# A Mamba skip weight loaded as a row, and dense feed-forward products of 512 columns with one loaded weight part

## The chip, the cores and the metric

The kernel runs on one core of one Trainium2 chip. The metric is device time in microseconds (us), the median of several runs. A core has five engines with an instruction queue each: TensorE (PE; its weight loads are shown apart as PEld), VectorE (DVE), ScalarE (ACT), GpSimd (POOL) and SyncE (SP, which here only issues transfers). Each queue is worked off in order; semaphores order the engines among each other. Sixteen DMA engines carry the transfers of all queues.

## The reference, cut to what matters

The program is two stacked blocks of two layers each on 256 tokens of width 1024. The change touches the three dense feed-forward layers (two in the first block, one in the second, all with a hidden width of 2816) and one vector of the Mamba layer.

```python
def swiglu_ffn(h, norm, w13, w2):                 # first block, both layers
    u = rms_norm(h, norm) @ w13
    return (silu(u[..., :2816]) * u[..., 2816:]) @ w2

def swiglu(h, w_gate, w_up, w_down):              # second block, first layer
    return (silu(h @ w_gate) * (h @ w_up)) @ w_down

# inside mamba2_mixer: ssm_d has 32 values, one for each head of 64 channels
    y = y + xf * d_skip[:, None]
```

All operands are 32-bit floats.

## The kernel before

**Split products.** TensorE works here in a rounded 32-bit format (fp32r), so each operand is split in a high part (rounded) and a low part (what the rounding left). `weights` (line 213) loads up to 128x2048 weights in one transfer of 1 MB from SP's queue into a buffer `raw`, then makes `wh` with four casts of 512 columns on ACT (line 227) and `wl` with four subtractions on DVE (line 228). `mm3` (lines 239 to 244) makes one product of the split operands as three: high weights by high operand (L242), high weights by low operand (L243), low weights by high operand (L244). Each of the three loads its 128x128 weights anew and passes 256 columns (the tokens) through them. I call the three a triple.

**A dense layer** (`ffn`, line 449). For each of 11 values of j, 256 hidden channels are made: `proj_fm` through `proj_steps` (line 249) for the gate weights, then for the up weights. Each such group is one `weights` call and 2 x 8 triples (two halves m of 128 channels, eight blocks k of the width) into one PSUM bank (`pa`, four banks of 512 columns; a group fills one). Then DVE multiplies gate and up by the row norm (`fg` L463, `fu` L465, both read PSUM), ACT makes the silu (L464), DVE the product (L466), and `split` makes `hidH` (ACT, L301) and `hidL` (DVE, L304). `out_proj` (line 379) then goes over four pairs of output blocks: 2 x 22 triples into one bank, one DVE addition of 512 columns to the residual `hT` (L395), and `norm_block` for the next layer. So a dense layer has 11 x 2 x 2 x 8 = 352 triples in gate and up and 4 x 2 x 22 = 176 in the output product: 528 in all, 1584 in the three layers.

**The normed operand.** `norm_block` (line 317) keeps the normed operand as tiles `xH` and `xL` of two blocks each; ACT writes `xH` (L326), DVE writes `xL` (L327).

**Buffers.** `wh` and `wl` have three buffers each in the dense layers and `raw` four (the `wider` context in `run`), so the parts of a third group can be made once the first group's triples have ended.

**The start.** `transpose_in` loads x, then SP issues the first weights of the even layer (`in_ev_w_in`). On POOL's queue `mamba_load` (line 646) loads three vectors of 32 values: two as rows broadcast to 128 partitions (L653) and the skip weight `ssm_d` as columns: `dcol` holds for 16 pairs of heads one head's value in the partitions 0 to 63 and the other's in 64 to 127, by two transfers (L657) that read 16 values at a stride of two for each of 64 partitions. `dcol` is first used in the Mamba layer (L777).

The order of the instructions on each engine is set by the framework's scheduler from priorities, when the program is built; it is not written out by hand.

Of the kernel before, what the change touches and what calls it, by code (L numbers as in the profile page):

```python
# [21 lines left out]
T = 256  # L22
# [28 lines left out]
def wait(tasks):  # L51
    while not all(t.done for t in tasks):
        yield


class Core:
# [192 lines left out]
    def proj_steps(s, src, c0, cn, X, evac, nk=8, tasks=None):  # L249
# [3 lines left out]
        while cn > 0:  # L253
            n = min(cn, 256)
            w = s.weights(src, 0, nk, c0, n)
            p = s.psum("a")
            nm = (n + 127) // 128
            for m in range(nm):
                mc = min(128, n - m * 128)
                for k in range(nk):  # L260
# [46 lines left out]
    def norm_open(s, gain, k0=0):  # L307
# [3 lines left out]
        N.H, N.L = [], []  # L311
        N.X = s.of_pairs(N.H, N.L)
# [4 lines left out]
    def norm_block(s, N, d0, src=None):  # L317
# [3 lines left out]
        N.H.append(s.t2([128, 2, T], "xH", F32R))  # L321
        N.L.append(s.t2([128, 2, T], "xL", F32R))
        for m in range(2):
            g = s.col(N.gain, N.k0 + d0 + m)
# [54 lines left out]
    def out_proj(s, src, Y, nk, nxt):  # L379

        moe = nxt == "moe"
        N = s.moe_open() if moe else s.norm_open(*nxt) if nxt else None
        block = s.moe_block if moe else s.norm_block
        for dp in range(4):
            p = s.psum("a")
            for k0 in range(0, nk, 8):
                n = min(8, nk - k0)
                w = s.weights(src, 128 * k0, n, dp * 256, 256)
                for m in range(2):
                    for k in range(n):  # L390
                        kk = k0 + k
                        s.mm3(p[:, m * 256:m * 256 + 256], [t[:, k, m * 128:m * 128 + 128] for t in w], Y(kk),
                              start=(kk == 0 and m == 0), stop=(kk == nk - 1))
            h = s.hT[:, 2 * dp:2 * dp + 2, :]
            s.nc.vector.tensor_add(h, h, p.rearrange("p (m t) -> p m t", m=2))  # L395
# [53 lines left out]
    def ffn(s, N, gate, up, gc, uc, w2, nxt):  # L449
# [4 lines left out]
        hH, hL = [], []  # L454
# [3 lines left out]
        for j in range(0, nf, 2):  # L458
            res = {}
            s.proj_fm(gate, gc + j * 128, 256, X, lambda _, p, n: res.__setitem__("g", p))  # L460
            s.proj_fm(up, uc + j * 128, 256, X, lambda _, p, n: res.__setitem__("u", p))
# [5 lines left out]
            hH.append(s.t2([128, 2, T], "hidH", F32R))  # L467
            hL.append(s.t2([128, 2, T], "hidL", F32R))
            s.split(u, hH[-1], hL[-1])
        return s.out_proj(w2, s.of_pairs(hH, hL), nf, nxt)  # L470
# [136 lines left out]
class Mamba:  # L607
# [38 lines left out]
    def mamba_load(s):  # L646
# [3 lines left out]
        vb = s.cp.tile([128, 2, 32], F32, name="ssmvb")  # L650
        for m, nm in enumerate(("ssm_dt_bias", "ssm_a_log")):
# [3 lines left out]
        sd = I["ssm_d"]  # L655
        for m in range(2):
            nc.gpsimd.dma_start(dcol[m * 64:m * 64 + 64],  # L657
# [1819 lines left out]
```

## Time and profile before

| | |
|---|---|
| median of 3 runs | 2528.38 us (2525.06 to 2529.42) |
| the profiled execution, its own time | 2530.27 us |
| span of its instructions | 2528.2 us |
| PE busy | 2329.6 us (92%) |
| the three dense layers, PE's stretch | about 382 to 574, 840 to 1030 and 1140 to 1328 us |
| PE's first product of weights | at 35.61 us |

The profile is of one execution. Its page gives busy time by engine, the span in 40 slices and the chain of work that ended last. The trace behind it is asked in views: instructions by line, a stretch in order of time, busy time by stretch, the transfers, and all instructions that touch one tile. A row with brackets says how long its engine sat idle ahead of it and what ended that. The time of a matmul includes its way through the array, so two neighbours overlap: the distance between two starts is what one costs in a full queue.

### The profile page before, as it was taken

To read this page: it belongs to the slowest core of one execution; us is meant where nothing else is said; L and a number is where in the kernel's file an instruction comes from. 1 tells how busy PE (TensorE), PEld (TensorE's weight loads), DVE (VectorE), ACT (ScalarE), POOL (GpSimd) and SP (SyncE) were. 2 spreads that over 40 slices of the span, in tenths; PEclk is the share of its full clock that TensorE was granted. 3 is DMA by queue.
4 is the path that set the end of the run, shared out by engine and by line. 5 is a ranking of instruction groups with operands and counts; after the bars stand their busy time and mean duration, and the time that the engine had idled before them with its cause. 6 is when DMAs were issued, how large, how long until landed. Compare 5 with 4: busy or idle time off the path is not lost.

```text
span 2528.2 us, 38949 instructions
## 1 busy us (share of the span) xinstructions
PE 2329.6 (92%) x15366; PEld 1917.4 (76%) x15366; DVE 1575.5 (62%) x2924; ACT 1201.5 (48%) x2075; POOL 88.3 (3%) x179
## 2 busy tenths in 40 slices
PE   4988999999998999989999998999999998788786
PEld 4877889999888999879999898787878883222222
DVE  4786677658986765766658885888888871000000
ACT  3554465445654544664446552777777661000000
POOL 3010110000001000000000000000000000000000
PEclk9998999999999999989999998999999999999999
DMA  6322245555434555515554300999999989999998
GB/s 116 118 77 68 74 161 174 175 183 156 134 117 151 152 177 178 177 58 184 182 169 151 101 18 31 376 343 355 359 357 343 345 308 412 410 411 410 411 412 319
DMA packets 266190, 559.55 MB, mean 221 GB/s; under 512 B 12751, under 2 KB 172510, under 8 KB 251662
## 3 DMA queue, kind: packets, MB, share of 16 engines
q1 hardware_dynamic: 264544, 555.71, 61.4%
q0 software_dynamic: 1328, 1.22, 1.0%
q8 instruction: 123, 2.02, 0.3%
q14 instruction: 69, 0.57, 0.1%
q10 hardware_dynamic: 126, 0.03, 0.0%
HBM read 555.88 MB, written 1.05 MB: 220 GB/s over the span
## 4 chain that ended last, share of the span: by engine, by line
PE 67%; DMA 14%; DVE 6%; ACT 3%; issue 2%; POOL 1%; SPq 0%; POOLq 0%; ACTq 0%; DVEq 0%
PE pa L243 16%; PE pa L244 16%; PE pa L242 15%; DMA wh<-in_o_moe_w_down_dram 4%; DMA raw<-in_o_moe_w_down_dram 2%; PE pb L243 2%; PE pb L244 2%; PE pb L242 2%; DMA raw<-in_o_moe_w_gate_dram 2%; DVE wl L228 2%; PE pb L1190 2%; DMA wl<-in_o_moe_w_gate_dram 2%; DMA wl<-in_o_moe_w_down_dram 2%; DMA raw<-in_o_moe_w_up_dram 2%; ACT wh L227 1%
## 5 line engine op out<-in xcount | busy, mean ns | idle before, releaser
L228 DVE TENSOR_TENSOR wl<-raw,wh 128x512 fp32r<-128x512 f32 (+2 forms) x940 | 879.5, 966 | 207.7 <-ACT wh L227 203.3
L227 ACT CAST wh<-raw 128x512 fp32r<-128x512 f32 (+2 forms) x940 | 746.1, 843 | 519.7 <-issue 269.8
L242 PE MATMUL pa<-xH,wh 128*128 128x256 f32 (+1 forms) x1936 | 554.5, 287 | 34.6 <-ACT xH L326 25.9
L243 PE MATMUL pa<-xL,wh 128*128 128x256 f32 (+1 forms) x1936 | 553.9, 287 | 1.3 <-DVE xL L327 1.3
L244 PE MATMUL pa<-xH,wl 128*128 128x256 f32 (+1 forms) x1936 | 553.2, 287 | 1.0 <-DVE wl L228 1.0
L242 PEld LDWEIGHTS pa<-xH,wh 128*128 128x128 f32 (+1 forms) x1936 | 373.2, 193 | 36.7 <-ACT xH L326 26.2
L243 PEld LDWEIGHTS pa<-xL,wh 128*128 128x128 f32 (+1 forms) x1936 | 373.1, 193 | 4.8 <-DVE xL L327 3.1
L244 PEld LDWEIGHTS pa<-xH,wl 128*128 128x128 f32 (+1 forms) x1936 | 373.2, 193 | 2.5 <-DVE wl L228 1.9
L2335 DVE SCALAR_TENSOR_TENSOR eh<-pa,slotrc,eh 128x512 f32<-128x512 f32 (+1 forms) x44 | 31.1, 727 | 372.6 <-PE pa L2319 365.8
L243 PE MATMUL pa<-wl,xe 128*128 128x512 f32 x448 | 177.7, 397 | 7.1 <-DVE wl L228 7.1
L244 PE MATMUL pa<-wh,xe 128*128 128x512 f32 x448 | 175.9, 393 | 0.0
L242 PE MATMUL pa<-wh,xe 128*128 128x512 f32 x448 | 166.5, 395 | 0.0
L242 PE MATMUL pa<-hidH,wh 128*128 128x256 f32 x528 | 149.4, 283 | 0.0
L244 PE MATMUL pa<-hidH,wl 128*128 128x256 f32 x528 | 149.4, 283 | 0.0
L243 PE MATMUL pa<-hidL,wh 128*128 128x256 f32 x528 | 149.4, 283 | 0.0
L2329 ACT ACTIVATE eh<-pa,slotrc 128x512 f32<-128x512 f32 (+1 forms) x44 | 28.5, 666 | 201.9 <-PE pa L2319 188.0
L2319 PE MATMUL pa<-raw,xf 128*64 128x512 f32 (+1 forms) x456 | 100.3, 542 | 21.6 <-DMA raw<-in_o_moe_w_up_dram 12.4
L243 PEld LDWEIGHTS pa<-wl,xe 128*128 128x128 f32 x448 | 84.7, 189 | 29.0 <-DVE wl L228 12.4
L244 PEld LDWEIGHTS pa<-hidH,wl 128*128 128x128 f32 x528 | 101.4, 192 | 0.0
L243 PEld LDWEIGHTS pa<-hidL,wh 128*128 128x128 f32 x528 | 101.4, 192 | 0.0
L242 PEld LDWEIGHTS pa<-hidH,wh 128*128 128x128 f32 x528 | 101.4, 192 | 0.0
L242 PEld LDWEIGHTS pa<-wh,xe 128*128 128x128 f32 x448 | 84.5, 189 | 17.1
(813 smaller groups left out, 3842.0 us busy)
## 6 DMA issues: line engine op xcount, KB each, us to landing
raw<-in_o_moe_w_down_dram SPq DMA_DIRECT2D x84, 1024.0 KB
raw<-in_o_moe_w_gate_dram SPq DMA_DIRECT2D x81, 1024.0 KB
raw<-in_o_moe_w_up_dram SPq DMA_DIRECT2D x80, 1024.0 KB
raw<-in_ffn_w_dram SPq DMA_DIRECT2D x60, 1024.0 KB
raw<-in_od_w_in_dram SPq DMA_DIRECT2D x20, 1024.0 KB
raw<-in_o_w_in_dram SPq DMA_DIRECT2D x16, 1024.0 KB
wl<-in_o_moe_w_gate_dram SPq DMA_DIRECT2D x16, 1024.0 KB
wh<-in_o_moe_w_up_dram SPq DMA_DIRECT2D x16, 1024.0 KB
```

The source lines that it names most:

```text
L227: nc.scalar.copy(H[:, c:e], raw[:, c:e])
L228: nc.vector.tensor_sub(L[:, c:e], raw[:, c:e], f(H[:, c:e]))
L242: mm(out, a[0], b[0], start=start, stop=False, skip_group_check=True)
L243: mm(out, a[0], b[1], start=False, stop=False, skip_group_check=True)
L244: mm(out, a[1], b[0], start=False, stop=stop, skip_group_check=True)
L1190: mm = lambda o, a, b, st=True, sp=True: nc.tensor.matmul(o, a, b, start=st, stop=sp, skip_group_check=True)
L2319: mm(p[0][64 * c:64 * c + 64, :hw], X[k0 + k][:, u], w[:, k, c * hw:c * hw + hw], start=start, stop=stop, skip_group_check=True)
L2329: nc.scalar.activation(out[-1], p, AF.Silu, scale=rc)
L2335: nc.vector.scalar_tensor_tensor(x, p, rc, x, op0=OP.mult, op1=OP.mult)
```

## The change

1. **Skip weights.** `ssm_d` is loaded as a third broadcast row of `ssmvb` (one transfer of 128x32 instead of the two), and `dcol` is made of that row by two small copies on DVE after the exponential of the second row, which now is written in place.
2. **Operand tiles.** The two parts of a block lie side by side in one tile (`Operand`): 256 columns of the high part, then 256 of the low part. `norm_block` writes `xHL` in that form for all its users; in the dense layers the hidden operand (`hid`) has it too.
3. **Products.** In gate, up and output product of the dense layers, the high weights are loaded once for both parts (one product of 512 columns), then the low weights for the high part (256 columns). The bank then holds the sum of high-by-high and low-by-high in its first half and high-by-low in its second.
4. **Adding the halves.** A bank now holds one m, so a group takes two banks. In gate and up, ACT copies the second half to a tile `pq` and DVE adds the first half, per m; `fg` and `fu` then read `pq`. In `out_proj` DVE adds both halves to `hT`, two additions of 256 columns per m. `hid` is split per m.

```diff
     def proj_steps(...):
             w = s.weights(src, 0, nk, c0, n)
...
+            if joint:
+                q = p = s.t2([128, 512], "pq")
...
+                if joint:
+                    b = s.psum("a")
+                    for k in range(nk):
+                        H, L = (t[:, k, m * 128:m * 128 + mc] for t in w)
+                        mm = s.nc.tensor.matmul
+                        mm(b[:mc], H, X.parts[k].rearrange("p a t -> p (a t)"), start=(k == 0), stop=False,
+                           skip_group_check=True)
+                        mm(b[:mc, :T], L, X(k)[0], start=False, stop=(k == nk - 1), skip_group_check=True)
+                    s.nc.scalar.copy(q[:mc, m * T:m * T + T], b[:mc, T:])
+                    s.nc.vector.tensor_add(q[:mc, m * T:m * T + T], b[:mc, :T], q[:mc, m * T:m * T + T])
...
     def out_proj(...):
-            p = s.psum("a")
+            p = [s.psum("a") for _ in range(2)]
...
-            h = s.hT[:, 2 * dp:2 * dp + 2, :]
-            s.nc.vector.tensor_add(h, h, p.rearrange("p (m t) -> p m t", m=2))
+            for m in range(2):
+                h = s.hT[:, 2 * dp + m, :]
+                for a in range(2):
+                    s.nc.vector.tensor_add(h, h, p[m][:, a * T:a * T + T])
...
     def ffn(...):
-            hH.append(s.t2([128, 2, T], "hidH", F32R))
-            hL.append(s.t2([128, 2, T], "hidL", F32R))
-            s.split(u, hH[-1], hL[-1])
+            for m in range(2):
+                hid.parts.append(s.t2([128, 2, T], "hid", F32R))
+                s.split(u[:, m, :], *hid(j + m))
...
     def mamba_load(s):
-        for m, nm in enumerate(("ssm_dt_bias", "ssm_a_log")):
+        for m, nm in enumerate(("ssm_dt_bias", "ssm_a_log", "ssm_d")):
...
-        for m in range(2):
-            nc.gpsimd.dma_start(dcol[m * 64:m * 64 + 64],
-                                bass.AP(tensor=sd.tensor, offset=sd.offset + m, ap=[[0, 64], [2, 16]]))
```

POOL's queue at the start, before (the names are tiles; L653 and L657 are `mamba_load`):

```order
L1061 IOTA tl__307 128x128
L653 DMA ssmvb<-in_ssm_dt_bias_dram 128x32
L653 DMA ssmvb<-in_ssm_a_log_dram 128x32
L657 DMA dcol<-in_ssm_d_dram 64x16x1 x2
L1677 DMA posi<-in_positions_dram 128x2x1
L1687 DMA mgn<-in_mla_q_hnorm_dram 128x64
```

and in the changed program:

```order
L1085 IOTA tl__307 128x128
L681 DMA ssmvb<-in_ssm_dt_bias_dram 128x32
L681 DMA ssmvb<-in_ssm_a_log_dram 128x32
L681 DMA ssmvb<-in_ssm_d_dram 128x32
L1704 DMA posi<-in_positions_dram 128x2x1
L1714 DMA mgn<-in_mla_q_hnorm_dram 128x64
```

At the same place in the queue one row transfer stands for the two element-wise ones; nothing else on POOL moves.

PE at the first dense layer's gate, before (two triples):

```order
L242 MATMUL pa_4139<-xH_4040,wh_4128 128x256
L243 MATMUL pa_4139<-xL_4041,wh_4128 128x256
L244 MATMUL pa_4139<-xH_4040,wl_4129 128x256
L242 MATMUL pa_4139<-xH_4040,wh_4128 128x256
L243 MATMUL pa_4139<-xL_4041,wh_4128 128x256
L244 MATMUL pa_4139<-xH_4040,wl_4129 128x256
```

and in the changed program (three blocks k):

```order
L279 MATMUL pa_4140<-xHL_4040,wh_4128 128x512
L281 MATMUL pa_4140<-xHL_4040,wl_4129 128x256
L279 MATMUL pa_4140<-xHL_4043,wh_4128 128x512
L281 MATMUL pa_4140<-xHL_4043,wl_4129 128x256
L279 MATMUL pa_4140<-xHL_4060,wh_4128 128x512
L281 MATMUL pa_4140<-xHL_4060,wl_4129 128x256
```

Two instructions with the same 768 columns stand for three.

DVE in the middle of a dense layer, before, for one gate group and one up group:

```order
L463 TENSOR_TENSOR fg_4513<-pa_4403,rB_4122 128x512
L228 TENSOR_TENSOR wl_4586<-raw_4584,wh_4585 128x512 x4
L465 TENSOR_TENSOR fu_4514<-pa_4464,rB_4122 128x512
L228 TENSOR_TENSOR wl_4657<-raw_4655,wh_4656 128x512
L466 TENSOR_TENSOR fu_4514<-fu_4514,fg_4513 128x512
L228 TENSOR_TENSOR wl_4657<-raw_4655,wh_4656 128x512 x2
L304 TENSOR_TENSOR hidL_4520<-fu_4514,hidH_4519 128x512
L228 TENSOR_TENSOR wl_4657<-raw_4655,wh_4656 128x512
```

and in the changed program (`pq` are the sums of the halves, L283):

```order
L283 TENSOR_TENSOR pq_4367<-pa_4368,pq_4367 128x256
L238 TENSOR_TENSOR wl_4522<-raw_4520,wh_4521 128x512
L283 TENSOR_TENSOR pq_4367<-pa_4387,pq_4367 128x256
L238 TENSOR_TENSOR wl_4522<-raw_4520,wh_4521 128x512 x3
L283 TENSOR_TENSOR pq_4418<-pa_4419,pq_4418 128x256
L491 TENSOR_TENSOR fg_4457<-pq_4367,rB_4122 128x512
L238 TENSOR_TENSOR wl_4585<-raw_4583,wh_4584 128x512
L283 TENSOR_TENSOR pq_4418<-pa_4438,pq_4418 128x256
L238 TENSOR_TENSOR wl_4585<-raw_4583,wh_4584 128x512
L493 TENSOR_TENSOR fu_4458<-pq_4418,rB_4122 128x512
```

The four additions stand between the weight subtractions, each where the half group that it reads ends on PE; on ACT the four copies (L282) stand between the casts in the same way.

## Rows read from the trace of the kernel before

**Rows 1.** The page: busy time by engine; the chain that ended last, by engine.

```profile
PE 2329.6 (92%) x15366; PEld 1917.4 (76%) x15366; DVE 1575.5 (62%) x2924; ACT 1201.5 (48%) x2075; POOL 88.3 (3%) x179
...
PE 67%; DMA 14%; DVE 6%; ACT 3%; issue 2%; POOL 1%; SPq 0%; POOLq 0%; ACTq 0%; DVEq 0%
```

**Rows 2.** In order of time, ACT and PE at the start (start, duration).

```profile
31.17 2.18 ACT L227 CAST wh<-raw 128x512 fp32r<-128x512 f32 x4 [28.45 <-DMA raw<-in_ev_w_in_dram]
34.01 1.14 ACT L227 CAST wh<-raw 128x512 fp32r<-128x512 f32 x2 [0.67 <-DMA raw<-in_ev_w_in_dram]
35.06 0.91 ACT L326 ACTIVATE xH<-hT,vc 128x256 fp32r<-128x256 f32 x2
...
35.61 0.80 PE L242 MATMUL pa<-xH,wh 128*128 128x256 f32 x2 [25.38 <-ACT xH L326]
```

**Rows 3.** Busy time by stretch at the start; last column GB/s moved.

```profile
core 0: us, PE busy (x) PEld busy (x) DVE busy (x) ACT busy (x) POOL busy (x), PEclk, DMA share, GB/s
...
8.00:11.00 3.00, 1.96 (x8) 1.53 (x8) 0.00 (x0) 0.00 (x0) 1.68 (x4) 1.00 1.30 310
11.00:16.00 5.00, 0.00 (x0) 0.00 (x0) 0.00 (x0) 0.00 (x0) 0.55 (x1) 1.00 1.32 12
...
21.00:26.00 5.00, 0.00 (x0) 0.00 (x0) 0.00 (x0) 0.00 (x0) 0.00 (x0) 1.00 0.00 0
...
28.00:31.00 3.00, 0.00 (x0) 0.00 (x0) 0.00 (x0) 0.00 (x0) 0.00 (x0) 1.00 0.65 209
```

**Rows 4.** Transfers begun from 10.9 to 21 us: queue, packets, MB, share.

```profile
q0 software_dynamic: 56, 0.01, 159.3%
q1 hardware_dynamic: 149, 0.15, 4.7%
```

**Rows 5.** All instructions of tile dcol, and of tile ssmvb: issue and landing.

```profile
L657 POOL DMA_DIRECT2D dcol<-in_ssm_d_dram x2: 834/842/850, 6.0 to 6.9; - x2
...
DMA to landing us min/median/max: 13.8/18.8/23.8
...
L653 POOL DMA_DIRECT2D ssmvb<-in_ssm_a_log_dram x1: 534/534/534, 5.5 to 5.5; - x1
...
DMA to landing us min/median/max: 6.2/6.4/6.6
```

**Rows 6.** Busy time by stretch: the first and third dense layer.

```profile
400.00:505.00 105.00, 105.00 (x878) 105.00 (x877) 68.48 (x110) 48.70 (x90) 0.00 (x0) 1.00 0.57 185
...
1160.00:1265.00 105.00, 105.00 (x877) 105.00 (x876) 68.00 (x109) 49.36 (x92) 0.00 (x0) 1.00 0.58 183
```

**Rows 7.** In order of time, PE in the first dense layer: two triples lie between.

```profile
429.97 0.28 PE L242 MATMUL pa<-xH,wh 128*128 128x256 f32 x1
...
430.69 0.28 PE L242 MATMUL pa<-xH,wh 128*128 128x256 f32 x1
```

**Rows 8.** In order of time, PE in the experts' layer: six 512-column products apart.

```profile
1699.63 0.39 PE L242 MATMUL pb<-wh,ehH 128*128 128x512 f32 x1
...
1700.99 0.62 PE L242 MATMUL pb<-wh,ehH 128*128 128x512 f32 x2
```

**Rows 9.** In order of time, DVE in the first dense layer.

```profile
453.57 0.69 DVE L465 TENSOR_TENSOR fu<-pa,rB 128x512 f32<-128x512 f32 x1 [2.32 <-PE pa L244]
...
459.33 0.69 DVE L463 TENSOR_TENSOR fg<-pa,rB 128x512 f32<-128x512 f32 x1 [1.46 <-PE pa L244]
```

**Rows 10.** Groups by line: instructions on 128x256 from PSUM; those split in two.

```profile
L1467 DVE TENSOR_TENSOR gy<-pb,ggate 128x256 f32<-128x256 f32 x8 | 3.0, 418 | 1.1 <-PE pb L1463 1.1
...
L301 ACT CAST xaH<-pb 128x256 fp32r<-128x256 f32 x8 | 3.0, 372 | 2.1 <-PE pb L600 2.1
...
L304 DVE TENSOR_TENSOR hidL<-fu,hidH 128x512 fp32r<-128x512 f32 x33 | 22.7, 687 | 0.0
...
L395 DVE TENSOR_TENSOR hT<-hT,pa 128x512 f32<-128x512 f32 x12 | 8.3, 688 | 14.9 <-PE pa L244 14.9
```

More of the change, by code (lines that the diff above doesn't have):

```diff
@@ L53, in wait, with __init__, __call__ @@
         yield
+class Operand:
+    def __init__(s):
+        s.parts = []
+    def __call__(s, k):
+        return s.parts[k][:, 0, :], s.parts[k][:, 1, :]
 class Core:
@@ L255, in proj_steps @@
             w = s.weights(src, 0, nk, c0, n)
-            p = s.psum("a")
             nm = (n + 127) // 128
+            if joint:
+                q = p = s.t2([128, 512], "pq")
+            else:
+                p = s.psum("a")
             for m in range(nm):
                 mc = min(128, n - m * 128)
-                for k in range(nk):
+                if joint:
[8 more added lines that the diff above has]
+                    s.nc.vector.tensor_add(q[:mc, m * T:m * T + T], b[:mc, :T], q[:mc, m * T:m * T + T])
+                for k in range(0 if joint else nk):
                     s.mm3(p[:mc, m * 256:m * 256 + 256],
@@ L310, in norm_open @@
         N.gain, N.k0 = gain, k0
-        N.H, N.L = [], []
-        N.X = s.of_pairs(N.H, N.L)
+        N.X = Operand()
         N.acc = s.t2([128, 2, T], "nacc")
@@ L320, in norm_block @@
         h = src[d0 // 2] if src is not None else s.hT[:, d0:d0 + 2, :]
-        N.H.append(s.t2([128, 2, T], "xH", F32R))
-        N.L.append(s.t2([128, 2, T], "xL", F32R))
         for m in range(2):
+            N.X.parts.append(s.t2([128, 2, T], "xHL", F32R))
             g = s.col(N.gain, N.k0 + d0 + m)
@@ L391, in out_proj @@
                         kk = k0 + k
-                        s.mm3(p[:, m * 256:m * 256 + 256], [t[:, k, m * 128:m * 128 + 128] for t in w], Y(kk),
-                              start=(kk == 0 and m == 0), stop=(kk == nk - 1))
-            h = s.hT[:, 2 * dp:2 * dp + 2, :]
-            s.nc.vector.tensor_add(h, h, p.rearrange("p (m t) -> p m t", m=2))
+                        H, L = (t[:, k, m * 128:m * 128 + 128] for t in w)
+                        mm(p[m], H, Y.parts[kk].rearrange("p a t -> p (a t)"), start=(kk == 0), stop=False,
+                           skip_group_check=True)
+                        mm(p[m][:, :T], L, Y(kk)[0], start=False, stop=(kk == nk - 1), skip_group_check=True)
+            for m in range(2):
+                h = s.hT[:, 2 * dp + m, :]
+                for a in range(2):
+                    s.nc.vector.tensor_add(h, h, p[m][:, a * T:a * T + T])
             if N:
@@ L453, in ffn @@
         s.norm_close(N)
-        hH, hL = [], []
+        hid = Operand()
         X = N.X
@@ L654, in mamba_load @@
         dcol = s.cp.tile([128, 16], F32, name="dcol")
[L655 to L659 removed]
+        s.ssm = dcol, vb, vb[:, 1, :]
     def mamba(s, N, nxt):
@@ L1597, in stream @@
                 yield start(3)
-                nc.scalar.activation(s.ssm[2], s.ssm[1][:, 1, :], AF.Exp)
+                dcol, vb, eA = s.ssm
+                nc.scalar.activation(eA, eA, AF.Exp)
+                for m in range(2):
+                    nc.vector.tensor_copy(dcol[m * 64:m * 64 + 64], vb[m * 64:m * 64 + 64, 2, m::2])
                 for g in beside:
```

13 lines of the change are left out of this document (6 added, 7 removed).

## The prediction

> **What bounds the kernel now.** I read the page's busy times and chain first, then the stretches, then single rows. PE is busy 92% of the span, and two thirds of the chain that ended last are PE's [rows 1]. But the share is a mean over stages with different limits, and the change touches two kinds of place.
>
> *The dense layers.* In a stretch of 105 us PE is busy all 105, with DVE at 68 and ACT at 49 [rows 6]. So PE's pace sets the time there, and weights come early enough. Two triples take 0.72 us from start to start [rows 7]: 0.36 us a triple, 120 ns a product of 256 columns. One value of j is 32 triples, 11.52 us.
>
> *The start.* PE's first product of weights starts at 35.61 us, after 25.38 us of idleness [rows 2]. PE waited for ACT, and ACT for the weights: 28.45 us for the first transfer and, since two casts of the second stand ahead of the operand, 0.67 us for the second at 34.01 [rows 2]. That is long for two transfers of 1 MB. The stretches show why: the core moved 310 GB/s from 8 to 11 us, then 12, then none from 21 to 26, and 209 again from 28 [rows 3]. While almost nothing moved, the DMA engines were not idle: of the transfers begun between 10.9 and 21 us, the 56 packets of POOL's queue with 0.01 MB took 159.3% of 16 engines over 10.1 us [rows 4], that is 1.593 x 10.1 = 16.1 us of every engine. POOL issued the two `dcol` transfers at 6.0 and 6.9 us, and they landed 13.8 and 23.8 us later, at about 20 and 31 us, just ahead of the first cast; the row transfer issued at 5.5 us landed after 6 to 7 us [rows 5]. So I take the two transfers of single elements to hold all engines for most of the time from 11 to 28 us.
>
> **The change part by part.**
>
> *Skip weights.* The two element-wise transfers go, one row transfer comes. What goes is at least 16.1 us of every engine [rows 4]. The other end: flow stopped for 17 us (11 to 28), and from 28 to 31 it ran at 209 instead of 310 GB/s [rows 3]; those 627 KB would take 2.0 instead of 3.0 us, so 18 us. I take 17. The new row is the like of the row next to it, done in 6 to 7 us [rows 5], and it joins the queue where the old ones stood, ahead of the positions and head gains that also gain. What is late next is still the second weights, then the 1.6 us from that landing to the first product (34.01 to 35.61), which stay. After that no engine waits for a clock time: all of the even layer hangs on these products, so I expect the shift to go through whole; the lower end is 13, if some other start-up load turns out late. `dcol` itself is made by two small copies long before its use, and costs nothing that shows.
>
> *Products.* There are 1584 triples. After the change each is one product of 512 columns and one of 256. The dense layers of before have no 512-column product; the experts' layer has, of the same type and with the same 128x128 weights, and six of them take 1.36 us, 227 ns each [rows 8]. So 256 columns more cost 107 ns, and of the 120 ns some 13 belong to the product as such. A triple becomes 227 + 120 = 347 ns, 13 less: 1584 x 13 = 20.6 us. The bounds are nothing (the pair costs what its columns cost at 120 ns per 256) and those 20.6; I take the upper, since the rows at both sizes are of the same form.
>
> The Trainium skill (TensorE: Matmul & The Clock Gate, Back-to-back issue gap) gives a warm product N/2.4 + 2.5 ns, which would be 109 and 216 ns. By it the change would save 2.5 ns a triple, 4 us in all, an estimate from that page. The rows show 120 and 227 ns, the same 107 for 256 columns but a fixed part of 13, and the measurement decides.
>
> *Adding the halves.* In each j DVE gets four additions of 256 columns that read PSUM, at 0.418 us by the nearest row, and two subtractions of 256 for one of 512 at 0.687 [rows 10]. The 105 us hold 9.11 values of j, so DVE works 7.51 us per j now [rows 6]; after it 7.51 + 1.67 + 0.15 = 9.33 of then 32 x 0.347 = 11.10 us, 84%. ACT gets four copies at 0.372 [rows 10] and one more cast of about that size: 5.34 + 1.86 = 7.2 us, 65%. Both stay under PE. What hides them: PE's weights are two groups ahead, and with four banks of 8 x 0.347 = 2.8 us PE asks for a bank again 8.3 us after it ended, while copy and addition take 0.8 us. The additions wait for PE in DVE's queue with the subtractions for later weights behind them, as `fg` and `fu` do now, for 2.32 and 1.46 us [rows 9]; those waits are DVE's spare time. If that cover were gone, it would be the slow rival below.
>
> *Output product.* Per pair of blocks four additions of 0.418 stand for one of 0.688 [rows 10]. Only those after the last product of a layer are on the path, two of them, about 0.15 us more; the first half's are done while PE works on the second. At a layer's beginning PE needs both parts of a block at once and reaches the last blocks sooner, since what it filled the wait with was 13 ns slower. I put 0.5 us a layer on both: 1.5 us.
>
> *Operand tiles.* The other users of `xHL` do the same products. The scheduler orders some casts and copies of the even layer differently; I put 0 on that, and 4 us either way in the range.
>
> *Sum.* 17 + 20.6 - 1.5 = 36.1 us. The profiled execution took 2530.3 us (span 2528.2 and 2.1 around it), so it would take 2494.2. It lies 1.9 us above the median of 2528.4, and the median goes to 2492.
>
> **The rivals.**
>
> *The packets are not the cause.* If the engines were held by something else at that time, or the row is as slow as the elements, the start gains nothing: 2528.4 - 19.1 = 2509. For it: 1024 elements of 4 bytes are little, and the hold is only told by the queue and the landing. Against: the row transfers of the same queue landed in 6 to 7 us, the elements at 20 and 31 [rows 5]. 6%. The Trainium skill (DMA: Bandwidth & Descriptors, Measured) has about 10.5 ns for a small packet, which makes 64 elements an engine 0.7 us, an estimate, and both transfers 1.3 us; by that page's price this rival would hold. Rows 4 show 16.1 us.
>
> *The fixed part does not go, or DVE is late in part.* If the pair takes its columns at the old rate, or DVE's additions eat the 13 ns, only the start remains: 2528.4 - 17 = 2511. For it: no row shows 512 and 256 columns in turn. Against: 120 and 227 ns on both sides. 8%.
>
> *Slower: DVE becomes the bound of the dense layers.* Place: each addition waits in DVE's queue for a copy that stands behind a weight cast on ACT. Price: a cast is 2.18/4 = 0.55 us [rows 2], the copy 0.372, so 0.92 a time and 3.7 per j; DVE then needs 9.33 + 3.7 = 13.0 us per j against 11.52 now. 33 x 1.5 = 49 us more, less 6.9 in the output product (528 x 13 ns) and 17 at the start: 2528.4 + 25 = 2553. It decides from 11.52 + (17 + 6.9 + 5)/33 = 12.4 us per j on. For it: DVE goes to 84% in strict order. Against: a queue that is behind PE finds the copy done, so it waits only while it is ahead, and it is ahead now [rows 9]. 4%.
>
> *Nothing moves.* Gains at the start that a later fixed wait gives back, with additions as in the second rival: 2528. 2%.
>
> **How the numbers follow.** The forecast has 80%: 2492. Its own spread is 13 to 19 at the start, 14 to 21 for the products and 4 for the order: 2483 to 2503. To leave out no more than 2 in 10 the range reaches to the first rival, 2482 to 2509. A measurement of this kernel can tell some 0.2%, 5 us, from no change. Faster: 80 + 6 + 8 = 94%; same 2%; slower 4%.
>
> **What would show it.** First product at 18 to 19 us, and no stretch of 4 us without data ahead of it. In the dense layers pairs of 0.347 us from start to start, j every 11.1 us, PE still busy throughout, DVE near 84%. A gap on PE that `wl` or a `pa` bank's release ends would show the slow rival; pairs of 0.36 us the second; a first product still after 30 us the first. I would be wrong altogether if the even layer ended at the same time in spite of an earlier start.

## The result, and the profile after

The changed kernel took 2502.18 us (median of 5 runs, 2497.18 to 2509.45), the kernel before beside it 2528.38 us (5 runs, 2522.44 to 2533.48): a ratio of 0.9895, with an interval of 0.9882 to 0.9908. That is 26.2 us less. The forecast was 36.1 us less, a time of 2492 in a range of 2482 to 2509. The sign and the range were right, the size was ten too large. The profiled execution of the changed kernel took 2497.18 us, the fastest of its five, where that of before took 2530.27: the two traces differ by 33 us, so the trace flatters the change by 7 us against the medians.

The page of the changed kernel, busy time by engine, the share of POOL's transfer queue, and one group of products (the last two columns are busy time with the mean of one in ns, and idle time ahead of them with what ended it), against [rows 1]:

```profile
PE 2307.2 (92%) x13782; PEld 1826.4 (73%) x13782; DVE 1629.0 (65%) x3127; ACT 1250.4 (50%) x2240; POOL 87.6 (4%) x178
...
q0 software_dynamic: 1296, 1.23, 0.2%
...
L279 PE MATMUL pa<-xHL,wh 128*128 128x512 f32 x1056 | 371.1, 397 | 6.6 <-DVE spu L649 6.6
```

PE has 1584 products fewer, DVE 53.5 us of work more, and POOL's queue took 0.2% of the engines' time instead of 1.0%. The last row holds the surprise: 6.6 us of idleness on PE, which the page puts down to a DVE instruction that has nothing to do with the dense layers. What PE waited for is told below, at the second layer's beginning.

**The start.** In order of time, ACT and then PE at the start (start, duration, and the idle time ahead with its releaser), against [rows 2]:

```profile
12.85 2.18 ACT L237 CAST wh<-raw 128x512 fp32r<-128x512 f32 x4 [10.13 <-DMA raw<-in_ev_w_in_dram]
16.11 1.14 ACT L237 CAST wh<-raw 128x512 fp32r<-128x512 f32 x2 [1.08 <-DMA raw<-in_ev_w_in_dram]
...
17.71 0.80 PE L252 MATMUL pa<-xHL,wh 128*128 128x256 f32 x2 [9.05 <-ACT xHL L348]
```

Busy time by stretch there (the last column is GB/s), against [rows 3]:

```profile
8.00:11.00 3.00, 0.66 (x5) 0.39 (x3) 0.00 (x0) 0.00 (x0) 1.07 (x3) 1.00 1.06 290
11.00:16.00 5.00, 0.00 (x0) 0.00 (x0) 2.50 (x6) 2.18 (x4) 0.00 (x0) 0.56 0.82 234
```

The landing of the three row transfers, of all instructions of tile ssmvb, against [rows 5]:

```profile
DMA to landing us min/median/max: 6.1/6.2/6.4
```

The hole in the flow of data is gone, the third row lands as fast as its neighbours, and the first product starts 17.9 us earlier.

**The dense layers.** Busy time by stretch in the three layers (length, then PE, PEld, DVE, ACT, POOL with their counts), against [rows 6]:

```profile
400.00:490.00 90.00, 90.00 (x521) 78.71 (x520) 71.23 (x138) 55.33 (x121) 0.00 (x0) 1.00 0.56 182
860.00:930.00 70.00, 70.00 (x406) 61.72 (x405) 54.50 (x107) 43.71 (x95) 0.00 (x0) 1.00 0.58 189
1125.00:1200.00 75.00, 75.00 (x426) 65.05 (x425) 59.28 (x115) 45.11 (x99) 0.00 (x0) 1.00 0.61 194
```

In the middle of the layers PE still sets the pace, and DVE is busy 78 to 79%. The group of the 132 additions says what they wait for in all:

```profile
L283 DVE TENSOR_TENSOR pq<-pa,pq 128x256 f32<-128x256 f32 x132 | 55.2, 420 | 1.2 <-ACT pq L282 1.2
```

They take 0.420 us each, as the nearest row had it [rows 10], and waited 1.2 us for ACT's copies altogether. But the counts differ: 521 products in 90 us are 172.7 ns each, 426 in 75 us are 176.1. In order of time, PE in the first layer, every other product left out:

```profile
429.62 0.40 PE L279 MATMUL pa<-xHL,wh 128*128 128x512 f32 x1
...
429.96 0.39 PE L279 MATMUL pa<-xHL,wh 128*128 128x512 f32 x1
...
430.31 0.40 PE L279 MATMUL pa<-xHL,wh 128*128 128x512 f32 x1
```

and in the third:

```profile
1159.74 0.40 PE L279 MATMUL pa<-xHL,wh 128*128 128x512 f32 x1
...
1160.09 0.40 PE L279 MATMUL pa<-xHL,wh 128*128 128x512 f32 x1
...
1160.45 0.40 PE L279 MATMUL pa<-xHL,wh 128*128 128x512 f32 x1
...
1160.80 0.40 PE L279 MATMUL pa<-xHL,wh 128*128 128x512 f32 x1
```

The first repeats every two pairs, 0.69 us (from the starts in ns: 350 and 343.5, mean 346.7). The third repeats every three, 1.06 us (350, 361 and 349, mean 353.3). I call them the two-pair and the three-pair pattern. In the second layer, behind the stall told below, every pair takes 346 or 347 ns: the same mean in another rhythm, which I count with the two-pair pattern. Behind its first 20 to 60 pairs, among which other products stand, a layer keeps its pattern to the last pair, output product included. In a second layer the pattern ahead of the stall can be another: here it was 350, 361 and 349. Against 360 ns a triple [rows 7] they save 13.3 and 6.7 ns.

**The second layer's beginning.** In order of time, PE, then ACT, then DVE:

```profile
819.22 0.28 PE L281 MATMUL pa<-xHL,wl 128*128 128x256 f32 x1
826.10 0.77 PE L279 MATMUL pa<-xHL,wh 128*128 128x512 f32 x1 [6.59 <-DVE spu L649]
826.66 0.41 PE L281 MATMUL pa<-xHL,wl 128*128 128x256 f32 x1
826.87 0.63 PE L279 MATMUL pa<-xHL,wh 128*128 128x512 f32 x1
...
827.51 0.63 PE L279 MATMUL pa<-xHL,wh 128*128 128x512 f32 x1
```

```profile
819.47 2.18 ACT L237 CAST wh<-raw 128x512 fp32r<-128x512 f32 x4 [2.46 <-issue]
821.66 1.28 ACT L642 ACT_TABLE_LOAD   x1
823.74 0.21 ACT L642 ACTIVATE spu<-spu 128x4 f32<-128x4 f32 x1 [0.80 <-DVE spu L641]
823.86 1.18 ACT L282 COPY pq<-pa 128x256 f32<-128x256 f32 x4
```

```profile
823.55 0.16 DVE L641 TENSOR_TENSOR spu<-spu,nlam 128x4 f32<-128x4 f32 x1
...
825.53 0.42 DVE L283 TENSOR_TENSOR pq<-pa,pq 128x256 f32<-128x256 f32 x1
```

PE had filled its four banks at 819 us. The first copy out of a bank started at 823.86 and the first addition at 825.53; the addition ended at 825.95, and PE went on at 826.10. So by these times it was the addition that gave PE a bank; the `spu` of PE's row (L649) stands right behind it in DVE's queue and ended at 826.02. Copy and addition came so late since ahead of them in the queues stand constants that the later even layer wants: rope tables (`rpAB`) and a softplus chain (`spu`), which `run` has made by `even2_ready` between the second cross-attention and this layer. The two queues hold each other up there: ACT's exponential at 823.74 waits for DVE's `spu` at 823.55.

The order on ACT counts as well. Ahead of the copies stand four casts of later weights (819.47). They go into the buffer of `wh` that the layer's second group had used, and so, after 2.46 us of idleness, could begin only when PE was done with that group, that is, when it had filled its fourth bank. In the first and third layer, where no constants are made, the first copies start 8.1 us after the layer's first product and stand ahead of those casts. The kernel before makes the same constants at the same place. There DVE's first reading of a bank came 20.5 us after the layer's first product (835.43), inside the 4 x 5.76 = 23.0 us that four banks covered, and PE did not stop:

```profile
855.95 0.68 DVE L463 TENSOR_TENSOR fg<-pa,rB 128x512 f32<-128x512 f32 x1
```

Busy time by stretch around the stall of the changed kernel (after the five engines' columns stands the granted clock):

```profile
813.00:819.00 6.00, 5.76 (x35) 4.89 (x34) 4.97 (x13) 3.87 (x7) 4.89 (x9) 1.00 0.98 288
819.00:826.00 7.00, 0.50 (x4) 0.17 (x2) 5.75 (x31) 5.70 (x11) 0.00 (x0) 0.86 1.03 295
826.00:831.00 5.00, 4.90 (x15) 4.21 (x16) 4.69 (x23) 1.07 (x3) 0.00 (x0) 0.52 0.40 141
```

After the idle time the granted clock was 0.52, near the level of 1.2 GHz, and a pair took 0.64 us (826.87 to 827.51). So the gap costs 6.6 us and some 2.3 behind it: the layer took 193.8 us where a layer of the same mean pair takes 184.9.

### The profile page after: what moved, and what is told of

Read it like the earlier page. It is cut to its first block, busy times and chain, and to the rows that moved or that the text cites. A ratio compares the mean times of both kernels' runs of the same rounds, so it can differ in the third digit from the quotient of the medians.

```text
span 2495.5 us, 36152 instructions
## 1 busy us (share of the span) xinstructions
PE 2307.2 (92%) x13782; PEld 1826.4 (73%) x13782; DVE 1629.0 (65%) x3127; ACT 1250.4 (50%) x2240; POOL 87.6 (4%) x178
## 4 chain that ended last, share of the span: by engine, by line
PE 65%; DMA 15%; DVE 7%; ACT 3%; issue 2%; POOL 2%; SPq 1%; POOLq 0%; ACTq 0%; DVEq 0%
PE pa L279 10%; PE pa L253 8%; PE pa L254 8%; PE pa L252 8%; PE pa L417 5%; PE pa L281 5%; DMA wh<-in_o_moe_w_down_dram 4%; PE pa L419 2%; DMA wh<-in_o_moe_w_gate_dram 2%; DVE wl L238 2%; DMA raw<-in_o_moe_w_down_dram 2%; PE pb L253 2%; PE pb L254 2%; PE pb L252 2%; DMA raw<-in_o_moe_w_gate_dram 2%
## 5 line engine op out<-in xcount | busy, mean ns | idle before, releaser
L279 PE MATMUL pa<-xHL,wh 128*128 128x512 f32 x1056 | 371.1, 397 | 6.6 <-DVE spu L649 6.6
L281 PE MATMUL pa<-xHL,wl 128*128 128x256 f32 x1056 | 295.2, 280 | 0.0
L252 PE MATMUL pa<-xHL,wh 128*128 128x256 f32 (+2 forms) x880 | 254.8, 291 | 15.6 <-ACT xHL L348 9.1
L254 PE MATMUL pa<-xHL,wl 128*128 128x256 f32 (+2 forms) x880 | 254.3, 290 | 3.6 <-DVE wl L238 3.6
L253 PE MATMUL pa<-xHL,wh 128*128 128x256 f32 (+2 forms) x880 | 253.9, 289 | 0.4 <-DVE xHL L349 0.3
L279 PEld LDWEIGHTS pa<-xHL,wh 128*128 128x128 f32 x1056 | 199.1, 189 | 53.0 <-issue 6.9
L281 PEld LDWEIGHTS pa<-xHL,wl 128*128 128x128 f32 x1056 | 200.2, 190 | 0.3
L417 PE MATMUL pa<-hid,wh 128*128 128x512 f32 x528 | 184.4, 394 | 0.0
L252 PEld LDWEIGHTS pa<-xHL,wh 128*128 128x128 f32 (+2 forms) x880 | 169.5, 193 | 17.7 <-ACT xHL L348 9.1
L254 PEld LDWEIGHTS pa<-xHL,wl 128*128 128x128 f32 (+2 forms) x880 | 169.6, 193 | 5.7 <-DVE wl L238 5.0
L253 PEld LDWEIGHTS pa<-xHL,wh 128*128 128x128 f32 (+2 forms) x880 | 169.7, 193 | 2.8 <-issue 1.2
L419 PE MATMUL pa<-hid,wl 128*128 128x256 f32 x528 | 147.5, 279 | 0.0
```

The lines of the kernel that those rows point to most:

```text
L252: mm(out, a[0], b[0], start=start, stop=False, skip_group_check=True)
L253: mm(out, a[0], b[1], start=False, stop=False, skip_group_check=True)
L254: mm(out, a[1], b[0], start=False, stop=stop, skip_group_check=True)
L279: mm(b[:mc], H, X.parts[k].rearrange("p a t -> p (a t)"), start=(k == 0), stop=False, skip_group_check=True)
L281: mm(b[:mc, :T], L, X(k)[0], start=False, stop=(k == nk - 1), skip_group_check=True)
L417: mm(p[m], H, Y.parts[kk].rearrange("p a t -> p (a t)"), start=(kk == 0), stop=False, skip_group_check=True)
```

## The experiments

Twelve experiments ran, with nine further kernels (e9 and e10 are the changed kernel again, e12 is e4 again). Ratios and gains are against runs of the kernel before made beside each: medians of 2528.4 us beside the changed kernel, 2529.5 beside e1 to e4, 2529.9 beside e5 to e8, 2528.1 beside e9 to e12. The table has the lengths of the three dense layers in the profiled execution (us, from the last product ahead of the layer to the last of its output product) and the pattern of each (in the second layer the one that it held to its end): 2 two-pair, 3 three-pair, o another order of products. The time is the median where there were several runs.

| kernel | time | first product | layer 1 | layer 2 | layer 3 |
|---|---|---|---|---|---|
| before | 2528.4 | 35.6 | 192.0 | 191.9 | 192.0 |
| changed | 2502.2 | 17.7 | 184.9 (2) | 193.8 (2) | 188.3 (3) |
| e1 row only | 2512.7 | 18.0 | 192.0 | 191.9 | 192.0 |
| e2 products only | 2520.4 | 35.0 | 188.3 (3) | 197.2 (3) | 188.4 (3) |
| e3 constants early | 2501.2 | 18.0 | 188.3 (3) | 184.9 (2) | 188.3 (3) |
| e4 eight banks | 2494.3 | 18.0 | 188.4 (3) | 184.7 (2) | 188.4 (3) |
| e5 sorted | 2503.4 | 17.6 | 186.2 (o) | 194.0 (o) | 186.2 (o) |
| e6 sorted, eight banks | 2498.9 | 18.4 | 186.4 (o) | 186.2 (o) | 186.4 (o) |
| e7 half the elements | 2521.2 (one run) | 27.6 | 192.0 | 191.9 | 192.0 |
| e8 more DVE work | 2516.1 (one run) | 18.0 | 190.1 | 198.6 | 191.0 |
| e9 changed, again | 2502.5 | 18.0 | 188.3 (3) | 197.4 (3) | 184.9 (2) |
| e10 changed, a third time | 2498.7 (one run) | 17.6 | 184.9 (2) | 197.3 (3) | 184.9 (2) |
| e11 mirrored, eight banks | 2492.2 | 18.0 | 185.7 (o) | 185.6 (o) | 185.7 (o) |
| e12 eight banks, again | 2495.7 | 18.3 | 188.3 (3) | 187.8 (3) | 188.3 (3) |

**e1, the row alone.** The diff's parts in `mamba_load` and behind the exponential, put into the kernel before.

> The kernel before with the row load of the skip weights alone (one broadcast row and two small copies on DVE in place of the two element-wise transfers); products as before. Theory: the element-wise transfers held the DMA engines and the start is worth the 17.9 us by which the changed kernel's first product came earlier. Expected: first product of weights at 17 to 19 us instead of 35.6, the dense layers unchanged at 192 us each, time 2528 - 18 = 2510 us (2507 to 2514). Rival: the shift at the start is given back before the first dense layer, because the even layer has a fixed wait; then the first dense layer begins nearer to 382 than to 364 us and the time stays above 2520.

2512.72 us (2510.92 to 2513.67), ratio 0.9931 [0.9918, 0.9943]. In order of time, its PE at the start:

```profile
18.00 0.79 PE L242 MATMUL pa<-xH,wh 128*128 128x256 f32 x2 [7.89 <-ACT xH L326]
```

The first product came 17.6 us earlier, the first dense layer 19.1 and the end 19.0, with three layers unchanged: the shift went through whole. In medians it was 16.8 us.

**e2, the products alone.** The changed kernel with the element-wise transfers of before.

> The changed kernel with the element-wise skip weights of before; the products of 512 columns stay. Theory: the two parts of the change add up, so the products are worth what the changed kernel gained beyond the start, 26.2 - 17.9 = 8 us, and the second dense layer has the stall of 6.6 us at its beginning here too. Expected: 2520 us (2516 to 2524), first product at 35 to 36 us, dense layers of about 185, 193 and 188 us. Rival: the stall in the second dense layer comes from a timing that only the earlier start brings about; then that layer takes about 186 us here and the time is about 2512.

2520.35 us (2516.2 to 2527.04), ratio 0.9960 [0.9945, 0.9974], 9.2 us less than before. 16.8 and 9.2 make 26.0, so the two parts add up to the 26.2 of the changed kernel. PE at its second dense layer's beginning:

```profile
852.25 0.77 PE L279 MATMUL pa<-xHL,wh 128*128 128x512 f32 x1 [6.59 <-DVE spu L649]
```

The stall is there to the same hundredth without the early start, so the rival falls. All three layers held the three-pair pattern, which I had not expected.

**e3, the constants moved.**

```diff
-                N = s.xattn(N, 1, ("ffn_norm", 8))
                 consts = s.even2_ready()
+                N = s.xattn(N, 1, ("ffn_norm", 8))
```

> The changed kernel with one call moved: the constants of the later even layer (rope tables, softplus chain) are made ahead of the second cross-attention, not between it and the second dense layer. Theory: in the changed kernel PE stood still for 6.6 us at 819 us and then ran slowly for some 7 us, because the first copies and additions of that layer stand behind these constants in the queues of ACT and DVE, and the four banks now hold 4 x 2.8 us of products instead of 4 x 5.8. Expected: no PE gap over 1 us at the beginning of the second dense layer, that layer at 185 to 188 us instead of 193.8, and if the constants cost nothing in the cross-attention a time of 2502 - 7 = 2495 us (2491 to 2499). Rival 1: the constants only move the stall, and the cross-attention grows by as much; then the layer is shorter and the time stays at 2502. Rival 2: the weights of the third group are what came late; then the gap stays.

2501.23 us (2496.62 to 2502.51), ratio 0.9879 [0.9865, 0.9894]: not to be told from the changed kernel. The second layer lost its gap and took 184.9 us. But the stretch between the first and second layer grew from 260.4 to 266.1 us, and PE shows where in the cross-attention:

```profile
788.44 3.58 PE L588 MATMUL pb<-ones,xsq 128*128 128x1 f32 x16 [4.86 <-ACT xsq L582]
```

4.86 us of waiting where the changed kernel waits 0.34 at the same step (775.89). In the second layer the first copies now come 8.0 us after the first product, as in the other two. Rival 1 holds: the constants, and the order that the scheduler makes with them, were the cause of the stall, and moved ahead they stop the next reader of ACT's queue, so that 5.7 of the 9 us came back.

**e4, eight banks.**

```diff
-                    b = s.psum("a")
+                    b = s.psum("ab"[m])
```

> The changed kernel with the two halves m of each gate and up group in banks of two pools (four banks each) instead of one, so that the products of four groups fit before the first copy, instead of two; the constants stay where they are. Theory: the banks ran out while copies and additions stood behind the constants. With eight banks PE has 8 x 2.8 = 22 us of room from the layer's beginning, while copies came after 17.4 us. Expected: the 6.6 us gap goes or falls under 1.5 us, the second dense layer takes 185 to 188 us, time 2494 us (2490 to 2499). Rival: the weights of the third group are late, not the banks; then the gap stays near 6 us and the time at 2502.

2494.25 us (2490.65 to 2498.01), ratio 0.9857 [0.9841, 0.9872]. Busy time by stretch at the second layer's beginning:

```profile
817.00:857.00 40.00, 39.87 (x233) 34.79 (x232) 36.90 (x115) 28.95 (x61) 5.70 (x9) 1.00 0.60 186
```

PE was busy 39.87 of 40 us at a clock of 1.00, with the constants where they had been, and the layer took 184.7 us. ACT shows that the copies did not come sooner for it:

```profile
834.40 0.36 ACT L282 COPY pq<-pa 128x256 f32<-128x256 f32 x1
```

That is the first copy of the layer, 20.5 us after its first product (813.92), later than the 17.3 us of the changed kernel, since the scheduler put four more casts ahead. Still PE did not stop, so it was the banks that ran out; the weights were not late. The first addition ended at 835.82 and PE wanted the ninth bank at 837.74, so eight banks had 1.9 us to spare.

**e5, sorted products.** In a bank, first the eight products of 512 columns, then the eight of 256.

```diff
                     for k in range(nk):
-                        mm(high part, 512 columns)
-                        mm(low part, 256 columns)
+                        mm(high part, 512 columns)
+                    for k in range(nk):
+                        mm(low part, 256 columns)
```

> The changed kernel with another order of the same products: in a bank all products of 512 columns come first, then all of 256, instead of one of each in turn. In the profiled runs so far each dense layer holds one of two repeating patterns from end to end: pairs of 350 and 343.5 ns in turn (346.7 a pair, layer 184.9 us) or 350, 361 and 349 (353.3 a pair, 188.3 us); which one differs from run to run. Theory: it is the change between the sizes that brings the slower pattern, and runs of one size go at 227 and 120 ns as in the experts' layer and in the kernel before. Expected: 347 ns a pair in all three layers in every run, 184 to 186 us for the first and third, the stall at the second layer's beginning as in the changed kernel, time 2497 us (2493 to 2501) and less spread from run to run than the changed kernel's 12 us. Rival: the patterns come from the sum of the columns or from the weight loads whatever the order; then layers of 188 us occur here too and the time is 2500 to 2504. A second rival: all operands of a layer's first bank are wanted earlier, and 1 us more is lost at each layer's beginning.

2503.41 us (2501.63 to 2511.3), ratio 0.9909 [0.9892, 0.9925]; a miss of 6 us. All layers became alike, at 186.2 us, so the patterns of 346.7 and 353.3 do belong to the strict alternation. But a pair cost 349.3 ns, not 347: after a change of size the first five products of 512 columns started 228 to 236 ns apart and only the later ones 227. And the runs still spread over 10 us, so the patterns are not the whole of the spread.

**e6, sorted with eight banks.** Both edits.

> The sorted order together with eight banks. Theory: the stall of the second dense layer (banks) and the slower pattern (order) are two separate losses and both go. Expected: three layers of 184 to 186 us, 2488 us (2485 to 2492). Rival: only the banks matter; then 2494 as with eight banks alone.

2498.91 us (2495.37 to 2501.97), ratio 0.9874 [0.9859, 0.9889]. That is above the range. The three layers took 186.2 to 186.4 us, close to what the theory has, yet the median fell by 4.5 us only, where e5's stall was worth 7.8 (194.0 to 186.2). In the profiled execution the stretch from the third layer to the experts took 257.7 us, against 249 to 253 in the other kernels; I did not find out why.

**e7, half of the elements.** The kernel before with one of the two element-wise transfers, the odd heads from the row.

```diff
-        for m in range(2):
-            nc.gpsimd.dma_start(dcol[m * 64:m * 64 + 64], ... offset=sd.offset + m, ap=[[0, 64], [2, 16]])
+        nc.gpsimd.dma_start(dcol[:64], ... offset=sd.offset, ap=[[0, 64], [2, 16]])
```

> The kernel before with one of the two element-wise transfers (the even heads, 64 partitions of 16 values), the odd heads from the row. Theory: the hold of the DMA engines is paid per element, 1024 elements instead of 2048. Expected: half of the shift, first product of weights at 26 to 28 us (35.6 with both, 18.0 with none), time about 2519. Rival: the hold is one fixed stall that any such transfer brings; then the first product stays at 34 to 36 us. A third way: the second transfer alone held the start; then 18 us.

2521.22 us in one run. Its PE at the start, and POOL's queue among the transfers begun from 10.9 to 21 us (packets, MB, share of 16 engines), against [rows 4]:

```profile
27.60 0.80 PE L242 MATMUL pa<-xH,wh 128*128 128x256 f32 x2 [17.53 <-ACT xH L326]
```

```profile
q0 software_dynamic: 66, 0.02, 88.7%
```

One transfer of the two, half of the elements, cost 9.6 of the 17.6 us, and the queue's share fell from 159.3 to 88.7%: the fixed stall and the third way fall. Whether the price is one by the element or by the transfer e7 does not show, since it halves both. In the trace of before each of the two transfers is 16 packets of 256 bytes, that is, 64 elements, and each packet took 5.8 to 9.6 us; the 16 other packets of 256 bytes in that queue took 0.02 us. So it is not the bytes.

**e8, more work for DVE.**

```diff
                     s.nc.vector.tensor_add(q[...], b[:mc, :T], q[...])
+                    for _ in range(2):
+                        s.nc.vector.tensor_copy(s.t2([128, T], "more"), b[:mc, :T])
```

> The changed kernel with two more DVE copies of 128x256 behind each addition of the halves in gate and up, of the same bank into tiles that nobody reads: eight more DVE instructions in each j. It measures how far the changed kernel is from DVE as the bound. DVE works 8.7 us per j in the changed kernel (71.2 of 90 us) where PE takes 11.1 to 11.3. Theory: room up to PE's pace, no more; 8 x 0.4 = 3.2 us make 11.9, so the dense layers' gate and up part becomes DVE's: about 11 x 0.7 = 8 us longer in each layer, 25 us in all, time about 2525 (2515 to 2540). Rival: waits in DVE's queue already fill it to PE's pace; then each copy shows whole, 3 x 11 x 3.2 = 105 us more. Second rival: the copies fit into room that is larger than it looks, and the time stays at 2502.

2516.07 us in one run, 14 more than the changed kernel's median where 25 were expected, at the lower end of the range. Busy time by stretch in its first dense layer:

```profile
405.00:490.00 85.00, 83.20 (x467) 70.91 (x466) 82.49 (x181) 49.01 (x108) 0.00 (x0) 1.00 0.56 183
```

DVE is busy 97%, and PE begins to wait, by its rows for 0.52 us on such a copy at 433.63 and again two j's later at 457.08. So a j took 23.45 / 2 = 11.7 us, against 11.1 in the changed kernel's first layer. Of it 97% are 11.4 us of DVE's work, 2.6 more than the changed kernel's 71.23 / 90 x 11.1 = 8.8. I had put 3.2 on the eight copies; behind one another they cost less than their 0.416 us. The room was thus about 2 us a j, what the copies cost less the 0.6 by which the j grew. This measure holds one thing more: the copies read the bank, and so also keep it from PE for longer. The three layers together took 579.7 us, against 567.0, 570.6 and 567.1 in the three profiles of the changed kernel.

**e9 and e10, the changed kernel again.** No edit.

> The changed kernel itself once more, for a second profile and for times beside the next runs. In its first profile the first and second dense layers held the pattern of 346.7 ns a pair and the third that of 353.3. Theory: which pattern a layer holds is settled by where its first products happen to fall, so that it differs from run to run of one and the same kernel; it is worth 528 x 6.7 ns = 3.5 us a layer and explains a good part of its spread of 12 us. Expected: another mix of layers at 184.9 and 188.3 us, median 2502 (2499 to 2505), the stall at the second layer's beginning again. Rival: the pattern belongs to the program; then the mix is the same as in the first profile.

> The same kernel a third time, for one more profile. By the theory of chance: the mix differs from at least one of the two others; by the rival: it is 184.9, 193.8 and 188.3 us in all three.

2502.46 us (2498.01 to 2506.7; ratio 0.9899 [0.9883, 0.9914]) and 2498.67 in one run. Layer by layer the patterns were 2, 2, 3 in the first profile, 3, 3, 2 in e9 and 2, 3, 2 in e10. So the program does not settle them; it is chance from run to run. The stall is not chance; first e9, then e10:

```profile
831.55 0.76 PE L279 MATMUL pa<-xHL,wh 128*128 128x512 f32 x1 [6.58 <-DVE spu L649]
```

```profile
827.25 0.77 PE L279 MATMUL pa<-xHL,wh 128*128 128x512 f32 x1 [6.59 <-DVE spu L649]
```

Against a layer of the same pattern the second layer lost 8.9, 9.1 and 9.0 us in the three profiles (193.8 - 184.9, 197.4 - 188.3, 197.3 - 188.3).

**e11, mirrored order with eight banks.** In every second block the product of 256 columns comes first.

```diff
+                        for part in ("HL", "LH")[k % 2]:
+                            mm(high part, 512 columns) if part == "H" else mm(low part, 256 columns)
```

> Eight banks, and in each second block k the product of 256 columns ahead of that of 512, so that sizes change half as often (512, 256, 256, 512). Theory: the slower pattern belongs to the strict alternation; with another rhythm the phases are others, and a pair costs 347 to 349 ns in every layer (the sorted order gave 349.3). Expected: layers of 184.5 to 186.5 us, 2493 us (2489 to 2497), no better than eight banks alone by more than its own spread. Rival: products that follow one of their own size cost less, under 344 ns a pair; then layers under 183 us and a time below 2488.

2492.24 us (2490.17 to 2492.94), ratio 0.9857 [0.9842, 0.9872]: the lowest median of the study, with a spread of 2.8 us. PE in its first layer (x2 are two in a row; their names, L281 for 512 and L284 for 256 columns, are this kernel's):

```profile
440.10 0.63 PE L281 MATMUL pb<-xHL,wh 128*128 128x512 f32 x2
440.57 0.40 PE L284 MATMUL pb<-xHL,wl 128*128 128x256 f32 x2
440.80 0.63 PE L281 MATMUL pb<-xHL,wh 128*128 128x512 f32 x2
```

Two pairs take 0.70 us from start to start, and all three layers took 185.6 or 185.7. The rival of 344 ns falls. From e4 and e12 it is not told apart with certainty: their medians lie 2 and 3.4 us higher, and the intervals of the ratio meet.

**e12, eight banks again.**

> The changed kernel with eight banks once more, now timed beside the changed kernel on the same chip. Theory: the stall at the second dense layer's beginning with the slow products behind it is worth 7 to 9 us of the time. Expected: 7 to 9 us below the changed kernel of this set, 2494 us (2491 to 2498), no gap over 1 us at that place. Rival: the first measurement of 2494 was luck of the patterns; then the two are within 3 us.

2495.68 us (2490.63 to 2499.67), ratio 0.9866 [0.985, 0.9882], 6.8 us below the changed kernel of the same set, just under the 7 to 9 expected. Its second layer's beginning:

```profile
818.00:858.00 40.00, 39.90 (x231) 34.59 (x230) 36.79 (x115) 28.65 (x61) 5.69 (x9) 1.00 0.59 181
```

The gap is gone here too. All layers held the three-pair pattern (the second from about its 55th pair on), so the first 2494 was not luck of the patterns.

## Why the prediction was right, and where its size was off

**What bounds the kernel.** Right for the start and for the middle of the layers. It was read in stretches from the middle of the first and third layer; the second layer's beginning, the one of the three at which constants stand in the queues of ACT and DVE, was not looked at.

**Skip weights, 17 us: right.** 17.2 to 18.0 us in the profiles with the row, and 19.0 at the end of e1, whose median gained 16.8. That the element-wise transfers held the engines was an inference from queue and landings; e1 shows it by taking them out alone, e7 by halving them. The first rival is out: removing them was worth 17.6 us. The price of 10.5 ns for a small packet (the Trainium skill, DMA: Bandwidth & Descriptors, Measured), by which both transfers would take 1.3 us, an estimate, does not give this. The prediction put an element for a packet; the trace has 64 elements in a packet and 8.0 us for one on the average.

**Products, 20.6 us: the step that failed, in two of its terms.** In the three profiles of the changed kernel the dense layers together gained 8.9, 5.3 and 8.8 us against before. First, the pair was put at 347 ns from two rows of single sizes. That is what the two-pair pattern has, but in the seven profiles with strict alternation and no added work (changed, e9, e10, e2, e3, e4, e12) 14 of 21 layers held the three-pair one, which gives half: 528 x 6.7 = 3.5 us a layer instead of 7.0. The text named that bound as "no row shows 512 and 256 columns in turn"; what it did not think of is that the same program has both values. The 2.5 ns by which a triple would shrink (the Trainium skill, TensorE: Matmul & The Clock Gate, Back-to-back issue gap, which gives it for an isolated product) lie below both.

Second, and larger: "What hides them". The working had PE come back to a bank 8.3 us after it ended while copy and addition take 0.8. That holds where copy and addition are next in their queues. At the second layer's beginning they are not: constants stand ahead, and the order on ACT puts the copies behind casts that wait for PE's second group. The first copy came 17.3 us after the layer's first product (806.5 to 823.86). Before, the first reading of a bank came 20.5 us after it and hid behind four banks of 5.76 us; now there are four banks of 2.8. It cost 9 us in every profile, which e4 and e12 took away by banks alone. It is the slow rival's mechanism, additions late in DVE's queue and PE out of banks, but once, at one place, by another cause than the one it named; and the sign that the text gave for it, a gap on PE that ends with a bank's release, is what showed it, though the row names the instruction behind the releasing one. Of the price it named nothing came: the 132 additions waited 1.2 us for ACT, where the rival had 0.92 us each.

**Adding the halves: right in the middle of the layers.** DVE at 78 to 79% (84 was forecast), ACT at 60 to 62% (65). The copies and additions do not show there.

**Layer ends, -1.5 us: too dark.** A layer of the two-pair pattern takes 184.9 us, of which 528 pairs at 346.7 ns are 183.1: 1.8 us beside the products, where before had 192.0 - 190.1 = 1.9. Nothing was added.

**The rest.** Outside start and dense layers the three profiles gained 6, 0.3 and 4.4 us. I put 0 on that. The stretch from the first product to the first dense layer took 343.4 to 344.7 us in the three profiles of the changed kernel, 346.6 in before, 345.1 in e1 and 345.9 to 349.3 in the other kernels with the new products, so executions differ there by as much as the gain. Whether the order of the even layer helped stays open.

**Together:** 17.8 for the start, 7.7 for the layers (the mean of 8.9, 5.3 and 8.8) and 3.6 for the rest are 29 us between the profiles, and 26.2 between the medians. With the 9 of the stall the medians would have given 35, and the kernels with eight banks, which have no stall, gained 35.3 (e4), 35.8 (e11), 32.4 (e12) and 31.0 (e6), against the 36.1 of the forecast. That the best of them come so near is in part luck. In e4's profile the start gave 17.6 and the layers 14.4 of 34.6 us, and 2.6 came from the rest, on which I had put 0; in e12's the layers gave 11.5. The spread of 14 to 21 us for the products was thus too narrow even without the stall. The time of 2502 lies inside the range, and just inside the 2483 to 2503 that the spreads of the terms gave, because the rest helped.

## What to carry to other kernels

Merging the products halved the time that the ring of banks covers (from 4 x 5.76 to 4 x 2.8 us), since a bank then held one half m instead of two. Before merging, look at every place where something unrelated stands in the queues that empty the banks, most of all where a stage begins, and not only at the steady middle. Moving such work ahead mostly changed who waited for it; more banks took the wait away. A transfer of a few kilobytes in single elements held up the first megabytes of weights here; load the row and take it apart on an engine that has time.

## What the runs showed of the hardware

- 2048 elements of 4 bytes, 16 in each of 128 partitions, held up the other queues for 17.6 us, and 1024 of them for 9.6 (27.6 against 18.0 us for the first product). A packet with 64 of these elements kept its engine for 5.8 to 9.6 us; other packets of 256 bytes in the same queue took 0.02.
- Alternating products of 512 and 256 columns fall into steady patterns with one of two means, 346.7 or 353.3 ns a pair, that a layer keeps behind its first 20 to 60 pairs. Which one is chance from layer to layer and run to run; three products of 256 columns (360 ns) show no such thing, nor do the sorted (349.3) and mirrored (348 to 349) order. What sets it was not found.
- After 6.6 us of idleness on PE the granted clock was 0.52 for the next 5 us, near the lower level of 1.2 GHz, and a pair took 0.64 us instead of 0.35.
